# A two-layer pooling and attention block on one core: another order of the attention's last products

## The chip, the core and the metric

The kernel runs on one core of a Trainium2 chip. Its engines run side by side, each through a queue of its own: TensorE (PE: matrix products into PSUM; PEld is its loading of weights), VectorE (DVE), ScalarE (ACT), GpSimd (POOL), and DMA queues (SP issues most transfers). The metric is the device time of one execution in microseconds (us), as the median of several runs. The profile is of one execution of its own; its span goes from the first to the last instruction.

## The reference

What is computed, for one sequence of 256 tokens with 1024 features, in float32, cut to its core:

```python
x = x + pool_mixer(rmsnorm(x, norm_mixer[0]), pool_w[0], pool_scale[0])   # running means over 2, 4, 8, 16 tokens
x = x + swiglu(rmsnorm(x, norm_ffn[0]), w_gate_up[0], w_down[0])          # d_ff = 2816
k, v = split(rmsnorm(x, kv_norm) @ w_kv)                                  # 16 heads of 64
q = rmsnorm(x, norm_mixer[1]) @ w_q[0]
o = softmax(q @ k.T / 8 + bias_by_distance, causal) @ v                   # block 256: all keys are in the own block
x = x + o @ w_o[0]
x = x + swiglu(rmsnorm(x, norm_ffn[1]), w_gate_up[1], w_down[1])
return rmsnorm(x, final_norm)
```

## The kernel before, in words

Activations lie with features on the 128 partitions, as `x[128, 8, 256]`: eight tiles of features by 256 tokens. Products are made in float32r out of halves: each operand is split into a high half (a rounded copy, made by ScalarE) and a low half (the rest, made by VectorE), and `mm3` sums three products, high by high (L72), high by low (L73) and low by high (L74). `mm2` makes the same three products in two matmuls, one of 512 columns (L79) and one of 256 (L80).

**Weights.** A plan lists all pieces of weights (1024 columns each) in the order of their use: ..., kq (two for each of the eight pairs of heads), wo (one for each of eight output tiles), gu1 (two for each of 22 gate and up tiles), dn1. A piece is loaded by SP, then split by ScalarE (L65, `whi`) and VectorE (L66, `wlo`) into one of five pairs of buffers (`HALVES = 5`). When TensorE's program comes to piece i, `weights` has the split of piece i + 4 written into the program; a split has to wait until the piece five places earlier is no longer used.

**Attention.** For each pair of heads p: `project(p)` makes keys and queries (eight k steps of six matmuls; L420, L425 and L427 then scale and split them), `scores(p)` makes q k, adds the bias (L447), and takes exponentials, sums and quotients (L450, L452, L455), `turn(p)` transposes the probabilities (L467) and splits them (L470, L471), `values(p)` multiplies them by v and splits the result into `oparts` (L484 the high half, L486 the low half). These stages are staggered: while pair p is projected, the scores of p - 1, the transposes of p - 2 and the values of p - 3 are made, at a place inside the eight k steps that `cut` sets.

**Output.** `attend(ms, ks)` adds, for each output tile m and pair k, the product of the wo piece of m with pair k's `oparts`. An output tile holds a PSUM bank and its split wo piece from its first k to its last. After k = 7, L501 adds the tile to `x`, L203 and L204 make the high and low half of the scaled `x` for the second feed-forward block, L196 squares it, and L198 adds the square to a running sum (tile 0 starts the sum, so there are seven L198).

**After that** the second feed-forward block runs over j = 0 to 21 (gate and up tiles) and k = 0 to 7. After the step j = 1, k = 1 TensorE multiplies the running sum of squares by a column of 1/1024 (L177, the mean square for the norm); VectorE adds epsilon (L169), GpSimd takes the power, and after j = 2, k = 0 the factor is spread over the partitions. L286 and L287 take a finished gate tile out of PSUM.

**Order.** TensorE's order is that of the code, written out by hand. On the other engines a scheduler sets the order when the program is built, with its own estimates of times; `high_priority` moves some instructions ahead. At run time each engine goes through its list in order.

Of the kernel before, what the change touches and what calls it, by code (L numbers as in the profile page):

```python
# [16 lines left out]
KT = D // P  # L17
# [19 lines left out]
def yoco_kernel(ctx, tc, x0, xs, pool_w, kq, wv, wo, rel_bias, gu, dn, onehot, mask, out):  # L37
# [10 lines left out]
    def bank():  # L48
        return psum.tile([P, 512], F32, name="bank", tag="bank")
# [19 lines left out]
    def mm3(o, w, a, first, last):  # L69

        (wh, wl), (ah, al) = w, a
        nc.tensor.matmul(o, wh, ah, start=first, stop=False)  # L72
        nc.tensor.matmul(o, wh, al, start=False, stop=False)  # L73
        nc.tensor.matmul(o, wl, ah, start=False, stop=last)  # L74
# [36 lines left out]
    def weights(name, key):  # L111
        i = used["n"]
        assert plan[i][:2] == (name, key), (plan[i][:2], name, key)
        used["n"] += 1
        prepare(i + HALVES)
        return ready.pop((name, key))
# [74 lines left out]
    def square(tag, m, eng=None):  # L191

        sq = work.tile([P, T], F32, name="sq", tag="sq")
        if m == 0:
            sq = acc[tag] = work.tile([P, T], F32, name="acc", tag="acc")
        nc.scalar.activation(sq, x[:, m, :], AF.Square)  # L196
        if m:
            (eng or nc.vector).tensor_tensor(acc[tag], acc[tag], sq, op=ALU.add)  # L198

    def split_x(m, v, s):  # L200

        g = vec[:, v, m:m + 1]
        nc.scalar.activation(act_hi[s][:, m, :], x[:, m, :], AF.Copy, scale=g)  # L203
        nc.vector.scalar_tensor_tensor(act_lo[s][:, m, :], x[:, m, :], g, act_hi[s][:, m, :].bitcast(F32),  # L204
                                       op0=ALU.mult, op1=ALU.subtract)
# [196 lines left out]
    def project(p, ks):  # L402
        if ks[0] == 0:
            proj[p] = [bank(), bank()]
        a = proj[p]
        for k in ks:
            if k % 4 == 0:
                kqw[0] = weights("kq", (p, k // 4))
            wh, wl = kqw[0]
            for u, s in enumerate("ab"):  # L410
                c = slice(k % 4 * T + u * P, k % 4 * T + (u + 1) * P)
                mm3(a[u][:, :T], (wh[:, c], wl[:, c]), (act_hi[s][:, k, :], act_lo[s][:, k, :]), k == 0, k == KT - 1)
        if ks[-1] != KT - 1:
            return
        t = work.tile([P, 2, T], F32, name="ev", tag="ev")
        q = [work.tile([P, T], F32R, name=f"q{s}", tag=f"q{s}") for s in "hl"]
        ks = kparts[p % 2]
        with tc.high_priority(URGENT):
            for u in (1, 0):
                nc.vector.tensor_tensor(t[:, u, :], a[u][:, :T], R2[:, u, :], op=ALU.mult)  # L420
            parts = [(q[0], q[1], t[:, 1, :])]
            for f, c in ((slice(0, 64), slice(0, T)), (slice(64, P), slice(T, 2 * T))):
                parts.append((ks[0][f, c], ks[1][f, c], t[f, 0, :]))
            for hi, lo, src in parts:
                nc.scalar.activation(hi, src, AF.Copy)  # L425
            for hi, lo, src in parts:
                nc.vector.tensor_tensor(lo, src, hi.bitcast(F32), op=ALU.subtract)  # L427
        kqs[p] = q, ks

    def scores(p):  # L430
        (qh, ql), (kh, kl) = kqs.pop(p)
        a = [bank(), bank()]
        kh0, kl0 = (v.rearrange("p (b k) -> p b k", b=2)[:, :, :P] for v in (kh, kl))
        mm3(a[0][:, :T], (qh[:, :P], ql[:, :P]), (kh0, kl0), True, True)
        mm3(a[1], (qh[:, P:], ql[:, P:]), (kh, kl), True, True)
        sn = work.tile([P, 2, 3 * P], F32, name="sn", tag="sn")
        pr = work.tile([P, 2, 3 * P], F32, name="pr", tag="pr")
        mx = work.tile([P, 2, 2], F32, name="mx", tag="mx")
        sm = work.tile([P, 2, 2], F32, name="sm", tag="sm")
        iv = work.tile([P, 2, 2], F32, name="iv", tag="iv")  # L440
        cols = (slice(0, P), slice(P, 3 * P))

        with tc.high_priority(URGENT):
            for b in range(2):
                h = 2 * p + b
                for t, (src, add) in enumerate(((a[0][:, b * P:(b + 1) * P], table[:, h, P:T]), (a[1][:, b * T:(b + 1) * T], table[:, h, :]))):
                    nc.vector.tensor_tensor_reduce(sn[:, b, cols[t]], src, add, -1.0, 3.0e38, ALU.add, ALU.min, mx[:, b, t:t + 1])  # L447
            for b in range(2):
                for t in range(2):
                    nc.scalar.activation(pr[:, b, cols[t]], sn[:, b, cols[t]], AF.Exp, bias=mx[:, b, t:t + 1], scale=-1.0,  # L450
                                         accum_out=sm[:, b, t:t + 1])
            nc.vector.reciprocal(iv, sm)  # L452
            for b in range(2):
                for t in range(2):
                    nc.gpsimd.tensor_scalar(pr[:, b, cols[t]], pr[:, b, cols[t]], iv[:, b, t:t + 1], 1.0, op0=ALU.mult, op1=ALU.mult)  # L455
        probs[p] = pr
# [3 lines left out]
    def turn(p):  # L460
        pr = probs.pop(p)
        c = [bank(), bank()]
        ph, pl = (work.tile([P, 2, 3 * P], F32R, name=f"p{s}", tag=f"p{s}", bufs=1) for s in "hl")
        for b in range(2):
            for i in range(3):

                nc.tensor.transpose(c[b][:, i * P:(i + 1) * P], pr[:, b, i * P:(i + 1) * P], ident)  # L467
        with tc.high_priority(URGENT):
            for b in range(2):
                nc.scalar.activation(ph[:, b, :], c[b][:, :3 * P], AF.Copy)  # L470
                nc.vector.tensor_tensor(pl[:, b, :], c[b][:, :3 * P], ph[:, b, :].bitcast(F32), op=ALU.subtract)  # L471
        pts[p] = ph, pl

    def values(p):
        ph, pl = pts.pop(p)
        o = bank()
        ob = o.rearrange("p (b q) -> p b q", b=2)
        for t, ks, dst in ((0, slice(0, T), ob), (1, slice(T, 3 * P), ob[:, :, P:])):
            vh, vl = (v[:, t, p * P:(p + 1) * P] for v in vparts)
            mm3(dst, (vh, vl), (ph[:, :, ks], pl[:, :, ks]), t == 0, t == 1)  # L480
        with tc.high_priority(URGENT):
            fs = [slice(64 * b, 64 * b + 64) for b in range(2)]
            for b, f in enumerate(fs):
                nc.scalar.activation(oparts[0][f, p, :], ob[f, b, :], AF.Copy)  # L484
            for b, f in enumerate(fs):
                nc.vector.tensor_tensor(oparts[1][f, p, :], ob[f, b, :], oparts[0][f, p, :].bitcast(F32), op=ALU.subtract)  # L486
# [3 lines left out]
    def attend(ms, ks):  # L490
        for k in ks:
            for m in ms:
                if m not in wos:
                    wos[m] = weights("wo", (m, 0))
                    wo_out[m] = bank()
                c = slice(k * P, (k + 1) * P)
                mm3(wo_out[m][:, :T], (wos[m][0][:, c], wos[m][1][:, c]), (oparts[0][:, k, :], oparts[1][:, k, :]),
                    k == 0, k == PAIRS - 1)
                if k == PAIRS - 1:
                    with tc.high_priority(URGENT):  # L500
                        nc.vector.tensor_tensor(x[:, m, :], wo_out[m][:, :T], x[:, m, :], op=ALU.add)  # L501
                        split_x(m, V_FFN1, "a")
                    square("ffn1", m)

    for p in range(PAIRS):
        cut = 4 if p > 2 else 6
        project(p, range(cut))
        if p >= 3:
            values(p - 3)
        if p >= 1:  # L510
            scores(p - 1)
        if p >= 2:
            turn(p - 2)
        project(p, range(cut, KT))

    attend((0,), range(5))
    values(PAIRS - 3)
    turn(PAIRS - 2)
    scores(PAIRS - 1)
    attend((0,), (5,))  # L520
    attend((1,), range(6))
    values(PAIRS - 2)
    attend((2,), range(6))
    turn(PAIRS - 1)
    attend((3,), range(6))
    values(PAIRS - 1)
    attend((0, 1, 2, 3), (6,))
    attend((0, 1, 2, 3), (7,))
    for m in range(4, KT):
        attend((m,), range(KT))  # L530

    last = const.tile([P, 2, KT, T], F32, name="last", tag="table")
# [97 lines left out]
```

## Time and profile before

| | before |
|---|---|
| median of 3 runs | 516.49 us (516.49 to 516.61) |
| the profiled execution | 516.71 us |
| its span | 515.0 us |
| around the span | 1.71 us |
| TensorE busy | 506.3 us, 98% |
| VectorE busy | 398.7 us, 77% |
| ScalarE busy | 303.3 us, 59% |
| mean granted TensorE clock | 0.997 |

The profiled execution is 0.22 us above the median. The end of a matmul is modelled in the profile and matmuls overlap, so what a stretch of matmuls takes is read from their starts. The attention's projections begin at about 229 us of the span, the first product of `attend` is at 292.3, the second feed-forward block begins at about 321.2.

### The profile page before, as it was taken

What the parts mean: (1) busy time and instruction counts of PE and PEld (TensorE: products, weight loads), DVE (VectorE), ACT (ScalarE), POOL (GpSimd) and SP (SyncE); (2) the same over time, 40 slices, a digit from 0 to 9 for tenths busy, and PEclk for the clock granted to TensorE, in tenths of its full rate; (3) what the DMA queues carried; (4) which work ended last, traced back from release to release, by engine and by line L of the source; (5) the groups of instructions that cost most, each with busy time, mean ns of one, the idle gap of its engine ahead of it and who ended that gap; (6) DMA issues with size and microseconds to landing.
All of it is one profiled execution on the core that took longest, in us unless ns stands there. A gap on an engine that the chain in (4) does not pass through costs nothing.

```text
span 515.0 us, 8445 instructions
## 1 busy us (share of the span) xinstructions
PE 506.3 (98%) x3084; PEld 450.9 (88%) x3084; DVE 398.7 (77%) x730; ACT 303.3 (59%) x556; POOL 43.9 (9%) x76
## 2 busy tenths in 40 slices
PE   8999999999999999999999999999999999999995
PEld 7888888888888888889999999888888888888895
DVE  6899878988876766657989849898888888865641
ACT  3967556565655554557777739576556565544421
POOL 4230300000000000201242410000000000000000
PEclk9999999999999999999999999999999999999998
DMA  8676999655657666565524215855555565666402
GB/s 295 244 221 170 226 215 340 208 184 176 185 159 206 183 192 215 186 196 168 156 93 158 92 39 166 263 184 187 186 197 184 188 188 164 189 179 191 114 1 82
DMA packets 26810, 92.28 MB, mean 179 GB/s; under 512 B 3088, under 2 KB 3248, under 8 KB 26768
## 3 DMA queue, kind: packets, MB, share of 16 engines
q1 hardware_dynamic: 25776, 88.78, 55.1%
q0 software_dynamic: 848, 2.57, 2.8%
q8 instruction: 24, 0.39, 0.3%
q10 hardware_dynamic: 144, 0.39, 0.2%
q14 instruction: 18, 0.15, 0.1%
HBM read 90.29 MB, written 1.44 MB: 178 GB/s over the span
## 4 chain that ended last, share of the span: by engine, by line
PE 56%; issue 36%; DVE 5%; DMA 1%; ACT 1%; POOL 0%; SPq 0%; POOLq 0%; DVEq 0%
PE bank L79 24%; PE bank L80 12%; PE bank L73 6%; PE bank L74 6%; PE bank L72 6%; DVE wlo L66 2%; PE bank L467 1%; DMA x<-in_xs 1%; DVE acta L204 1%; DVE acc L198 0%; DVE x L501 0%; ACT early L225 0%; DVE early L233 0%; PE bank L177 0%; PE bank L245 0%
## 5 line engine op out<-in xcount | busy, mean ns | idle before, releaser
L66 DVE TENSOR_TENSOR wlo<-raw,whi 128x1024 fp32r<-128x1024 f32 x168 | 202.5, 1206 | 59.6 <-ACT whi L65 52.2
L65 ACT ACTIVATE whi<-raw 128x1024 fp32r<-128x1024 f32 x168 | 174.0, 1037 | 116.5 <-PE bank L79 88.5
L79 PE MATMUL bank<-actb,whi 128*128 128x512 f32 x352 | 124.4, 396 | 0.0
L79 PE MATMUL bank<-acta,whi 128*128 128x512 f32 x352 | 123.6, 394 | 0.0
L79 PE MATMUL bank<-big,whi 128*128 128x512 f32 x330 | 114.5, 390 | 0.0
L80 PE MATMUL bank<-actb,wlo 128*128 128x256 f32 x352 | 98.2, 279 | 0.0
L80 PE MATMUL bank<-acta,wlo 128*128 128x256 f32 x352 | 98.2, 279 | 0.0
L80 PE MATMUL bank<-big,wlo 128*128 128x256 f32 x330 | 93.0, 282 | 0.0
L79 PEld LDWEIGHTS bank<-actb,whi 128*128 128x128 f32 x352 | 66.0, 187 | 16.2 <-DVE ev L287 0.6
L79 PEld LDWEIGHTS bank<-acta,whi 128*128 128x128 f32 x352 | 66.0, 187 | 15.6
L79 PEld LDWEIGHTS bank<-big,whi 128*128 128x128 f32 x330 | 61.9, 188 | 13.0
L80 PEld LDWEIGHTS bank<-actb,wlo 128*128 128x128 f32 x352 | 66.0, 188 | 0.0
L80 PEld LDWEIGHTS bank<-acta,wlo 128*128 128x128 f32 x352 | 66.0, 187 | 0.0
L80 PEld LDWEIGHTS bank<-big,wlo 128*128 128x128 f32 x330 | 62.4, 189 | 0.0
L286 ACT ACTIVATE ev<-bank 128x256 f32<-128x256 f32 x88 | 33.2, 379 | 47.6 <-PE bank L80 47.6
L287 DVE TENSOR_TENSOR ev<-bank,ev 128x256 f32<-128x256 f32 x88 | 36.8, 419 | 13.1 <-ACT ev L286 13.1
L288 DVE TENSOR_TENSOR ev<-ev,R 128x256 f32<-128x256 f32 x88 | 36.8, 423 | 2.6
L455 POOL TENSOR_SCALAR pr<-pr,iv 128x128 f32<-128x128 f32 (+1 forms) x32 | 21.1, 677 | 68.0 <-DVE iv L452 40.1
L73 PE MATMUL bank<-big,whi 128*128 128x256 f32 x86 | 24.1, 281 | 0.2 <-DVE big L486 0.2
L72 PE MATMUL bank<-big,whi 128*128 128x256 f32 x86 | 24.1, 280 | 0.0
L74 PE MATMUL bank<-big,wlo 128*128 128x256 f32 x86 | 24.0, 279 | 0.0
L291 DVE TENSOR_TENSOR h<-sg,ev 128x256 f32<-128x256 f32 x44 | 18.5, 423 | 4.8 <-ACT sg L289 0.5
(135 smaller groups left out, 674.5 us busy)
## 6 DMA issues: line engine op xcount, KB each, us to landing
raw<-in_gu SPq DMA_DIRECT2D x88, 512.0 KB, 4.1
raw<-in_dn SPq DMA_DIRECT2D x32, 512.0 KB, 3.6
raw<-in_kq SPq DMA_DIRECT2D x16, 512.0 KB, 4.4
raw<-in_dn SPq DMA_DIRECT2D x16, 384.0 KB, 3.6
raw<-in_wv SPq DMA_DIRECT2D x8, 512.0 KB, 4.3
raw<-in_wo SPq DMA_DIRECT2D x8, 512.0 KB, 3.5
table<-rows POOLq DMA_DIRECT2D x8, 256.0 KB, 16.9
early<-in_pool_w SPq DMA_DIRECT2D x4, 256.0 KB, 4.8
```

The lines of the kernel that those rows point to most:

```text
L65: nc.scalar.activation(hi[:, :cols], raw[:, :cols], AF.Copy)
L66: nc.vector.tensor_tensor(lo[:, :cols], raw[:, :cols], hi[:, :cols].bitcast(F32), op=ALU.subtract)
L72: nc.tensor.matmul(o, wh, ah, start=first, stop=False)
L73: nc.tensor.matmul(o, wh, al, start=False, stop=False)
L74: nc.tensor.matmul(o, wl, ah, start=False, stop=last)
L79: nc.tensor.matmul(o, wh, a.rearrange("p a t -> p (a t)"), start=first, stop=False)
L80: nc.tensor.matmul(o[:, :T], wl, a[:, 0, :], start=False, stop=last)
L286: nc.scalar.activation(t[:, u, :], a[u][:, T:], AF.Copy)
L287: nc.vector.tensor_tensor(t[:, u, :], a[u][:, :T], t[:, u, :], op=ALU.add)
L288: nc.vector.tensor_tensor(t[:, u, :], t[:, u, :], R, op=ALU.mult)
L291: nc.vector.tensor_tensor(h, sg, t[:, 1, :], op=ALU.mult)
L455: nc.gpsimd.tensor_scalar(pr[:, b, cols[t]], pr[:, b, cols[t]], iv[:, b, t:t + 1], 1.0, op0=ALU.mult, op1=ALU.mult)
```

## The change

```diff
     for p in range(PAIRS):
-        cut = 4 if p > 2 else 6
+        cut = 4 if p > 3 else 6
         project(p, range(cut))
         if p >= 3:
             values(p - 3)
...
         project(p, range(cut, KT))
 
-    attend((0,), range(5))
+    attend((0, 1), range(5))
     values(PAIRS - 3)
     turn(PAIRS - 2)
     scores(PAIRS - 1)
-    attend((0,), (5,))
-    attend((1,), range(6))
+    attend((0, 1), (5,))
+    attend((2,), range(6))
     values(PAIRS - 2)
-    attend((2,), range(6))
+    attend((3,), range(6))
     turn(PAIRS - 1)
-    attend((3,), range(6))
+    attend((0, 1, 2, 3), (6,))
     values(PAIRS - 1)
-    attend((0, 1, 2, 3), (6,))
-    attend((0, 1, 2, 3), (7,))
-    for m in range(4, KT):
+    attend((4,), range(7))
+    attend((0, 1, 2, 3, 4), (7,))
+    for m in range(5, KT):
         attend((m,), range(KT))
```

In the loop only the pass p = 3 changes: it makes six k steps of its projection, not four, before the values of pair 0, the scores of pair 2 and the transposes of pair 1. In the straight part two output tiles instead of one are begun before `values(5)`; tile 2 and tile 3 each move one place ahead; the products with pair 6 stand before `values(7)`; a fifth tile makes seven products behind `values(7)`, and five tiles end together instead of four. All products are the same in number, form and kind.

The scheduler places VectorE's and ScalarE's work anew. Three places of that follow. In the names a number tells tiles of one kind apart.

The first is VectorE's list where the first output tiles are added to `x`. Before:

```order
L486 TENSOR_TENSOR big_2193<-bank_3454,big_2193 64x256 x2
L501 TENSOR_TENSOR x_71<-bank_3284,x_71 128x256
L501 TENSOR_TENSOR x_71<-bank_3360,x_71 128x256
L501 TENSOR_TENSOR x_71<-bank_3396,x_71 128x256
L66 TENSOR_TENSOR wlo_3355<-raw_2993,whi_3354 128x1024
L204 SCALAR_TENSOR_TENSOR acta_134<-x_71,acta_134 128x256 x3
L501 TENSOR_TENSOR x_71<-bank_3435,x_71 128x256
L66 TENSOR_TENSOR wlo_3391<-raw_3036,whi_3390 128x1024
```

And of the change:

```order
L486 TENSOR_TENSOR big_2193<-bank_3466,big_2193 64x256 x2
L501 TENSOR_TENSOR x_71<-bank_3284,x_71 128x256
L501 TENSOR_TENSOR x_71<-bank_3294,x_71 128x256
L501 TENSOR_TENSOR x_71<-bank_3385,x_71 128x256
L66 TENSOR_TENSOR wlo_3289<-raw_2993,whi_3288 128x1024
L66 TENSOR_TENSOR wlo_3380<-raw_3036,whi_3379 128x1024
L204 SCALAR_TENSOR_TENSOR acta_134<-x_71,acta_134 128x256 x3
L501 TENSOR_TENSOR x_71<-bank_3421,x_71 128x256
```

`raw_2993` and `raw_3036` are the wo pieces of tiles 5 and 6: both splits stand now before the first L204, where one did.

The second is VectorE's list around the end of the sum of squares. `sq_3658` is the square of tile 7, the last one; `wlo_3713` is the split of gu piece 6 (tile j = 3, first half), `wlo_3689` that of gu piece 5. Before:

```order
L198 TENSOR_TENSOR acc_3484<-acc_3484,sq_3621 128x256
L66 TENSOR_TENSOR wlo_3667<-raw_3394,whi_3666 128x1024
L198 TENSOR_TENSOR acc_3484<-acc_3484,sq_3658 128x256
L66 TENSOR_TENSOR wlo_3689<-raw_3433,whi_3688 128x1024
L287 TENSOR_TENSOR ev_3781<-bank_3664,ev_3781 128x256
L66 TENSOR_TENSOR wlo_3713<-raw_3517,whi_3712 128x1024
L169 TENSOR_SCALAR rv_3729<-bank_3726 128x2
```

And of the change:

```order
L66 TENSOR_TENSOR wlo_3689<-raw_3419,whi_3688 128x1024
L198 TENSOR_TENSOR acc_3512<-acc_3512,sq_3621 128x256
L66 TENSOR_TENSOR wlo_3713<-raw_3481,whi_3712 128x1024
L198 TENSOR_TENSOR acc_3512<-acc_3512,sq_3658 128x256
L287 TENSOR_TENSOR ev_3781<-bank_3664,ev_3781 128x256
L169 TENSOR_SCALAR rv_3729<-bank_3726 128x2
```

The last L198 stood before the splits of gu pieces 5 and 6; it stands behind both now, and the first L287 behind both too, where it stood between them.

The third is ScalarE's list at the same place; `bank_3664` is the first gate tile of the feed-forward block. Before:

```order
L65 ACTIVATE whi_3666<-raw_3394 128x1024
L196 ACTIVATE sq_3621<-x_71 128x256
L203 ACTIVATE acta_134<-x_71 128x256
L196 ACTIVATE sq_3658<-x_71 128x256
L65 ACTIVATE whi_3688<-raw_3433 128x1024
L286 ACTIVATE ev_3781<-bank_3664 128x256
L65 ACTIVATE whi_3712<-raw_3517 128x1024
L286 ACTIVATE ev_3781<-bank_3665 128x256
```

And of the change:

```order
L65 ACTIVATE whi_3688<-raw_3419 128x1024
L196 ACTIVATE sq_3584<-x_71 128x256
L196 ACTIVATE sq_3621<-x_71 128x256
L286 ACTIVATE ev_3781<-bank_3664 128x256
L65 ACTIVATE whi_3712<-raw_3481 128x1024
L196 ACTIVATE sq_3658<-x_71 128x256
L286 ACTIVATE ev_3781<-bank_3665 128x256
```

The square of tile 7 stood before the high halves of gu pieces 5 and 6 and before the first L286; it stands behind them now.

## Rows read from the trace of the kernel before

**Rows 1.** The page's first part: busy us, share of the span and instructions.

```profile
PE 506.3 (98%) x3084; PEld 450.9 (88%) x3084; DVE 398.7 (77%) x730; ACT 303.3 (59%) x556; POOL 43.9 (9%) x76
```

**Rows 2.** List of waits, weight loads: total us, times, longest.

```profile
PEld bank L73 <- DVE big L427: 0.5, 2, 0.3
...
PEld bank L73 <- DVE big L486: 0.4, 1, 0.4
```

**Rows 3.** Timeline, TensorE, third pair's scores: start, duration, engine, line, instruction.

```profile
253.34 0.28 PE L72 MATMUL bank<-big,qh 128*128 128x256 f32 x1
253.63 0.39 PE L73 MATMUL bank<-big,qh 128*128 128x256 f32 x1
253.86 0.28 PE L74 MATMUL bank<-big,ql 128*128 128x256 f32 x1
```

**Rows 4.** Timeline, TensorE: last pair's scores, and products behind the last transposes.

```profile
295.69 0.36 PE L72 MATMUL bank<-big,qh 128*128 128x256 f32 x1
...
296.38 0.28 PE L74 MATMUL bank<-big,ql 128*128 128x256 f32 x1
...
303.43 0.36 PE L72 MATMUL bank<-big,whi 128*128 128x256 f32 x1
303.64 0.28 PE L73 MATMUL bank<-big,whi 128*128 128x256 f32 x1
```

**Rows 5.** Timeline, TensorE, from the first product with the last values.

```profile
308.06 0.28 PE L72 MATMUL bank<-big,whi 128*128 128x256 f32 x1
308.58 0.39 PE L73 MATMUL bank<-big,whi 128*128 128x256 f32 x1 [0.24 <-DVE big L486]
308.80 0.28 PE L74 MATMUL bank<-big,wlo 128*128 128x256 f32 x1
...
313.47 0.28 PE L72 MATMUL bank<-big,whi 128*128 128x256 f32 x1
```

**Rows 6.** By stretches: length, busy us of PE, PEld, DVE, ACT, POOL, clock, DMA.

```profile
313.00:317.00 4.00, 4.00 (x37) 4.00 (x36) 4.00 (x8) 4.00 (x9) 0.00 (x0) 1.00 0.70 232
```

**Rows 7.** Timeline, VectorE, from the first tile's addition to the first L287.

```profile
309.11 1.13 DVE L501 TENSOR_TENSOR x<-bank,x 128x256 f32<-128x256 f32 x3 [0.59 <-PE bank L74]
310.16 1.21 DVE L66 TENSOR_TENSOR wlo<-raw,whi 128x1024 fp32r<-128x1024 f32 x1
...
326.23 0.41 DVE L198 TENSOR_TENSOR acc<-acc,sq 128x256 f32<-128x256 f32 x1
326.57 1.21 DVE L66 TENSOR_TENSOR wlo<-raw,whi 128x1024 fp32r<-128x1024 f32 x1
327.70 0.41 DVE L287 TENSOR_TENSOR ev<-bank,ev 128x256 f32<-128x256 f32 x1
```

**Rows 8.** Timeline, ScalarE, the same stretch.

```profile
309.00 1.06 ACT L65 ACTIVATE whi<-raw 128x1024 fp32r<-128x1024 f32 x1 [1.37 <-PE bank L73]
...
326.62 0.39 ACT L286 ACTIVATE ev<-bank 128x256 f32<-128x256 f32 x1 [1.51 <-PE bank L80]
```

**Rows 9.** Timeline, TensorE, the statistics.

```profile
328.17 0.50 PE L177 MATMUL bank<-mean,acc 128*128 128x1 f32 x4
```

**Rows 10.** VectorE's and TensorE's timelines: pair 3's low half, its use; last values.

```profile
260.86 1.07 DVE L427 TENSOR_TENSOR big<-ev,big 64x256 fp32r<-64x256 f32 x2
...
262.26 0.28 PE L73 MATMUL bank<-big,qh 128*128 128x256 f32 x1
...
306.55 0.28 PE L74 MATMUL bank<-ph,big 128*128 128x256 f32 x1
...
307.66 0.86 DVE L486 TENSOR_TENSOR big<-bank,big 64x256 fp32r<-64x256 f32 x2 [2.67 <-ACT big L484]
```

**Rows 11.** TensorE's last matmuls, and stretches to the end (columns as in Rows 6).

```profile
507.82 1.29 PE L552 MATMUL bank<-ident,last 128*128 128x128 f32 x10
...
511.00:512.00 1.00, 0.00 (x0) 0.00 (x0) 0.00 (x0) 0.00 (x0) 0.00 (x0) 0.99 1.04 404
512.00:513.00 1.00, 0.00 (x0) 0.00 (x0) 0.00 (x0) 0.00 (x0) 0.00 (x0) 0.50 1.04 412
```

## Prediction

> **What bounds the kernel now.** The page is read first [rows 1]: TensorE is busy for 506.3 of 515.0 us, so time is gained or lost only where TensorE waits. The list of TensorE's waits comes next. Near the attention it holds three, all at L73, the first product of a group that needs a low half: two for the low half of k, which L427 writes, and one for the low half of the attention output, which L486 writes [rows 2]. TensorE's timeline then gives what each costs, from the starts of consecutive matmuls. Undisturbed, 40 matmuls of 256 columns go from 308.80 to 313.47, 0.117 us each [rows 5].
> - Third pair's scores: 253.34 to 253.86 is 0.52 us for two steps that take 0.23 undisturbed. Cost 0.29 [rows 3].
> - Last pair's scores: 295.69 to 296.38, 0.69. The first step after a block of transposes takes 0.21 even without a wait (303.43 to 303.64), so 0.33 is the undisturbed time and 0.36 the cost [rows 4].
> - Seventh products after the last values: 308.06 to 308.80, 0.74 against 0.23. Cost 0.50 [rows 5].
>
> Together 1.15 us. That is the most that the three edits can give back, and just over 0.2% of 516.5 us (1.03 us), about what a measurement of this kernel can tell from no change.
>
> Then the other engines, from 309 us on. VectorE is busy for 4.00 us of 313 to 317 [rows 6]; it works without a gap from its first L501 at 309.11 to its first L287 at 327.70 [rows 7]. In that block stand 8 L501 (output added to x), 8 L204 (low half of the next activation), 7 L198 (sum of squares) and 9 L66 (low halves of weights: wo 5 to 7, gu pieces 0 to 5). The sum of squares is the operand of L177 at 328.17 [rows 9]. The last L198 ends at 326.64, so the sum is there 1.5 us before TensorE comes to L177; everything behind that matmul stands in the same queue. This margin is the place that decides.
>
> **The change, part by part.** No instruction is added or removed on TensorE; only places change.
>
> *Third pair, cut 6 for 4.* Two k steps (12 matmuls, 1.40 us) go ahead of values(0) and scores(2), so the wait of 0.29 goes. But scores(2) and turn(1) now come 1.40 us later against the end of project(3), and VectorE's work for them is pushed against L420 and L427 of pair 3. Before, that low half ends at 261.93 and is wanted at 262.26, a margin of 0.33 [rows 10]. Following ACT and VectorE through the new order (two L447, L486, two L447, L471, L452, L420, L66, L427), I get it ready about 0.1 us after it is wanted, which with the restart below costs about 0.2. Bounds of the gain: 0 and 0.29; I take 0.1.
>
> *Two tiles ahead of the last scores.* Fifteen matmuls (1.76 us) of tile 1 move ahead, past a wait of 0.36, which goes. Behind the scores there is then less between values(5) and its use in attend((0, 1), (5,)). The low half of the last values was there at 308.52 (L486 runs 0.86 from 307.66), 1.9 us after the step of their last matmul, which starts at 306.55 [rows 10]; values(5) is followed by 1.84 us of transposes, scores and one product. So about 0.1 may be waited here, and 0.1 more for the restart. Bounds 0.16 and 0.36; I take 0.2. Together **G = 0.3**, between 0.16 and 0.65.
>
> *Fifth tile between values(7) and its use.* Seven products of tile 4, 21 matmuls or 2.46 us, replace a wait of 0.50. The wait goes, as the low half is ready 1.9 us after the values. But tile 0's last product, and with it the start of VectorE's block, moves from 308.80 to 308.80 + 2.46 - 0.50 = 310.76 (less G), 1.96 later. And there are only five buffers of split weights, all held now by tiles 0 to 4: wo 5 can be split only after tile 0's last product, as before, where ScalarE starts it at 309.00 [rows 8]. Before, tile 4's eight steps (2.8 us) lay between that and tile 5. Now only the last products of tiles 1 to 4 do.
>
> *First new wait, tile 5.* VectorE starts at 311.07, does three L501 (1.05 us, 309.11 to 310.16 [rows 7]), then the L66 of wo 5 (1.21): 313.33. TensorE wants the low half five steps after tile 0's last matmul, at 310.76 + 5 x 0.352 = 312.52. It waits 0.9, plus 0.1: after a wait, the next matmul comes 0.22 later instead of 0.117 [rows 3, 5].
>
> *Second new wait, the statistics.* VectorE's block starts 1.96 later, at 311.07, and the order shows one more L66 in it (gu piece 6) before the last L198: 1.13 us (326.57 to 327.70 [rows 7]). It ends at 311.07 + 18.59 + 1.13 = 330.79; with the overlap of neighbours (0.07), the release (0.06) and the restart (0.1), TensorE is 331.02 - 328.17 = 2.85 us later behind L177 than before, less G. The wait at tile 5 is inside this sum, not beside it: VectorE's block doesn't wait for tiles 5 to 7 in my following of it, and TensorE itself reaches L177 at about 328.6, so it stands there some 2.3 us.
> The second bound drops the backlog. In the new order ScalarE has L286 of the first gate tile, then L65 of gu piece 6, ahead of the last square, and that L65 needs a buffer free that TensorE holds until the first gate tile ends. From L286's start (326.62 before [rows 8]): 0.39 + 1.06 + 1.21 + 0.41 = 3.07 until the sum is there, where L177 comes 1.55 after it. That alone is a stall of 1.5, on top of 0.97 at tile 5 and less 0.50 and G: 2.0 - G with 0.1 for the restart. Both lie on the same side; I take the first, as VectorE's queue is full.
>
> After L177 nothing gives this back: the list of TensorE's waits has none later in the program at which spare time could be absorbed, and the order of all engines there is as before.
>
> Sum against the profiled execution: 516.71 + 2.85 - 0.3 = 519.26. The median shown is 0.22 below that execution: **519.0**.
>
> The Trainium skill (Perfetto Trace Analysis, Identifying the Most-Contended Engine) has the engine of highest occupancy optimized first, by closing its gaps; over the span that is TensorE with 98% against VectorE's 77%, and by this the change would give 1.15 us, 515.3. The rows of the stretch differ: there VectorE has no idle time at all.
>
> **The rivals.**
> - *Faster.* The three waits go and nothing takes their place: 516.49 - 1.15 = 515.3. TensorE would come to L177 at 328.17 - 1.15 = 327.0 and need the sum by then, 3.6 us earlier than I get it (330.9 - G). For it: all of this is in the shade of TensorE's own work on average. Against it: the added L66 stands ahead of the last L198 in the order, and both bounds exclude it.
> - *No change.* The wait at tile 5 comes but the statistics are in time: -1.15 + 0.97 = -0.2, 516.3. It needs a VectorE block shorter by the 2.3 us of the stall: each of its ten L66 would have to take 0.9 instead of 1.13.
> - *The clock falls.* At the end of the program the last matmuls end at 509.11 and the granted clock stays at 1.00 until about 511.98, then is 0.50 (1.2 of 2.4 GHz) until the end, 3.0 us [rows 11]. A stall of 2.3 us is shorter than those 2.9, so I expect no fall. If it fell for such 3.0 us, it would cost half of them: 519.0 + 1.5 = 520.5. The Trainium skill (TensorE: Matmul & The Clock Gate, HAM oscillation) tells of kernels whose waits between bursts of matmuls put TensorE back to half its clock, each time; that speaks for this rival.
> - *The early waits come back whole* (G = 0): 519.3; kept whole (G = 0.65): 518.7. Both are within the forecast.
>
> **How the numbers follow.** Forecast 0.80, clock 0.07, no change 0.08, faster 0.05. The forecast's own range is 518.1 (the second bound, 2.0 - 0.65 = 1.35 up, is 517.8; with half of the backlog 518.1) to 519.4 (G = 0); instructions on VectorE a little slower than in the rows would add 0.2. To leave out no more than 2 in 10 I give 517.8 to 519.7. Slower by over 0.2%: 0.87; within: 0.08; faster: 0.05.
>
> **What would show it.** In the profile after: TensorE's waits list holds L177 <- VectorE L198 with some 2.3 us, and L74 <- L66 with about 0.9; L73 <- L486 is gone; the wait at the third pair's scores has moved to the fourth's or is gone. VectorE is without a gap from its first L501 to the last L198, 19.7 us. The clock is 1.00 behind L177. I am wrong if L177 starts within 0.5 us of the matmul before it: then the last L198 was not late, and either VectorE ran its block faster or the buffers were freed in another order than I read.

## The result, and the profile after

The changed kernel takes 520.94 us (median of 6 runs, 519.02 to 521.59) against 516.49 before (6 runs, 516.39 to 516.97). The ratio is 1.0076, 95% interval 1.0064 to 1.0087: slower by 0.76%, 4.4 us. The direction and the two new waits came as forecast; the time lies 1.2 us above the range.

The page of the profiled execution (520.91 us, span 519.2), first part, answers to [rows 1]: the work is the same, 1.7 us more of TensorE's time is spent on it, and the rest of the 4.2 us is standing.

```profile
PE 508.0 (98%) x3084; PEld 452.2 (87%) x3084; DVE 399.8 (77%) x730; ACT 303.4 (58%) x556; POOL 44.0 (8%) x76
```

The list of TensorE's waits (total us, times, longest) has two new lines, each at the place forecast:

```profile
PE bank L177 <- DVE acc L198: 2.1, 1, 2.1
...
PE bank L74 <- DVE wlo L66: 0.7, 1, 0.7
PE bank L73 <- DVE big L427: 0.2, 1, 0.2
```

Before, L73 <- L486 was the only line of that list from 230 us on, with 0.2; it is gone. [rows 2] show the list of weight loads, and there the line is left with half of its 0.4. It now belongs to the products with pair 5, and no longer to the last values:

```profile
PEld bank L73 <- DVE big L486: 0.2, 1, 0.2
```

TensorE's timeline at the two, answering to [rows 5] and [rows 9]. The third product of tile 5 comes 0.99 us after the second (0.117 undisturbed), the next one 0.22 later: 0.97 lost. L177 comes 2.39 us after the matmul before it.

```profile
312.18 0.28 PE L73 MATMUL bank<-big,whi 128*128 128x256 f32 x1
313.17 0.39 PE L74 MATMUL bank<-big,wlo 128*128 128x256 f32 x1 [0.71 <-DVE wlo L66]
313.39 0.28 PE L72 MATMUL bank<-big,whi 128*128 128x256 f32 x1
...
328.33 0.28 PE L80 MATMUL bank<-acta,wlo 128*128 128x256 f32 x1
330.72 0.66 PE L177 MATMUL bank<-mean,acc 128*128 128x1 f32 x4 [2.10 <-DVE acc L198]
331.23 0.78 PE L79 MATMUL bank<-acta,whi 128*128 128x512 f32 x1
331.81 0.41 PE L80 MATMUL bank<-acta,wlo 128*128 128x256 f32 x1
332.02 0.63 PE L79 MATMUL bank<-acta,whi 128*128 128x512 f32 x1
332.45 0.41 PE L80 MATMUL bank<-acta,wlo 128*128 128x256 f32 x1
332.66 0.63 PE L79 MATMUL bank<-acta,whi 128*128 128x512 f32 x1
```

The last four rows show something else: a pair of L79 and L80 takes 0.64 us there, where it takes 0.35 undisturbed (the L80 before the first row starts at 327.98, the first row at 328.33). The stretches of the same trace (length, busy us of PE, PEld, DVE, ACT, POOL, granted clock, DMA) say why: TensorE is idle from 328.6 to 330.7 with the clock at 1.00, and the clock is at 0.50, 1.2 of 2.4 GHz, from 331.1 (the 0.86 of the second stretch) to 334.5, after TensorE has gone back to work.

```profile
328.60:330.70 2.10, 0.01 (x1) 0.00 (x0) 2.10 (x5) 0.20 (x1) 0.00 (x0) 1.00 0.86 250
330.70:331.30 0.60, 0.58 (x5) 0.59 (x5) 0.30 (x1) 0.00 (x0) 0.00 (x0) 0.86 0.83 239
331.30:334.50 3.20, 3.20 (x11) 2.72 (x11) 0.97 (x4) 0.53 (x1) 0.70 (x1) 0.50 0.88 307
334.50:336.00 1.50, 1.50 (x11) 1.32 (x10) 0.94 (x1) 0.53 (x1) 0.00 (x0) 0.98 0.09 38
```

Some 3.4 us at half clock are 1.7 us of work lost, as an estimate. By the starts it is 1.6: the five pairs from 331.23 to 334.57 take 3.34 us, and 1.76 undisturbed. Of the six executions four have a mean granted clock of 0.993 to 0.995 and times of 520.91 to 521.59; the other two have 0.996 and 0.997 and take 519.02 and 519.68. So the time has two levels, near 519.3 and near 521.2, and the median is of the upper one.

VectorE's timeline answers to [rows 7]: the block starts at 310.85, and the last L198 stands behind the split of gu piece 6. From the first L501 to the end of the last L198 it takes 19.8 us, with no gap over 0.06.

```profile
310.85 1.13 DVE L501 TENSOR_TENSOR x<-bank,x 128x256 f32<-128x256 f32 x3 [1.17 <-PE bank L74]
...
329.10 1.22 DVE L66 TENSOR_TENSOR wlo<-raw,whi 128x1024 fp32r<-128x1024 f32 x1
330.24 0.42 DVE L198 TENSOR_TENSOR acc<-acc,sq 128x256 f32<-128x256 f32 x1
330.57 0.42 DVE L287 TENSOR_TENSOR ev<-bank,ev 128x256 f32<-128x256 f32 x1
```

The wait at the third pair's scores of [rows 3] is gone (254.58 to 254.82 is 0.24 for two steps), and one stands at the fourth's, where [rows 10] had none: 261.66 to 262.33 is 0.67 for two steps of 0.23, a loss of 0.44. The last pair's scores no longer wait (297.40 to 297.73 is 0.33, as undisturbed), but the first products with pair 5 behind them do: 298.55 to 298.96, 0.41 for 0.23, a loss of 0.18.

```profile
261.66 0.28 PE L72 MATMUL bank<-big,qh 128*128 128x256 f32 x1
262.11 0.38 PE L73 MATMUL bank<-big,qh 128*128 128x256 f32 x1 [0.16 <-DVE big L427]
262.33 0.28 PE L74 MATMUL bank<-big,ql 128*128 128x256 f32 x1
...
298.55 0.28 PE L72 MATMUL bank<-big,whi 128*128 128x256 f32 x1
298.74 0.38 PE L73 MATMUL bank<-big,whi 128*128 128x256 f32 x1
298.96 0.28 PE L74 MATMUL bank<-big,wlo 128*128 128x256 f32 x1
```

### The profile page after: what moved, and what is told of

Read it like the earlier page. It is cut to its first block, busy times and chain, and to the rows that moved or that the text cites. A ratio compares the mean times of both kernels' runs of the same rounds, so it can differ in the third digit from the quotient of the medians.

```text
span 519.2 us, 8447 instructions
## 1 busy us (share of the span) xinstructions
PE 508.0 (98%) x3084; PEld 452.2 (87%) x3084; DVE 399.8 (77%) x730; ACT 303.4 (58%) x556; POOL 44.0 (8%) x76
## 4 chain that ended last, share of the span: by engine, by line
PE 61%; issue 35%; DVE 2%; ACT 1%; POOL 0%; POOLq 0%; DVEq 0%
PE bank L79 24%; PE bank L80 12%; PE bank L73 7%; PE bank L74 7%; PE bank L72 7%; PE bank L467 1%; PE bank L142 1%; PE bank L220 1%; DVE wlo L66 0%; ACT early L225 0%; PE bank L177 0%; DVE acc L198 0%; PE bank L245 0%; DVE last L569 0%; POOL r_mix L171 0%
## 5 line engine op out<-in xcount | busy, mean ns | idle before, releaser
L79 PE MATMUL bank<-acta,whi 128*128 128x512 f32 x352 | 125.1, 397 | 0.0
L79 PE MATMUL bank<-actb,whi 128*128 128x512 f32 x352 | 124.4, 395 | 0.0
L79 PE MATMUL bank<-big,whi 128*128 128x512 f32 x330 | 114.5, 390 | 0.0
L80 PE MATMUL bank<-acta,wlo 128*128 128x256 f32 x352 | 98.8, 281 | 0.0
L80 PE MATMUL bank<-actb,wlo 128*128 128x256 f32 x352 | 98.2, 279 | 0.0
L80 PE MATMUL bank<-big,wlo 128*128 128x256 f32 x330 | 93.0, 282 | 0.0
L79 PEld LDWEIGHTS bank<-acta,whi 128*128 128x128 f32 x352 | 66.8, 190 | 16.0
L79 PEld LDWEIGHTS bank<-actb,whi 128*128 128x128 f32 x352 | 66.0, 187 | 16.0 <-DVE ev L287 0.6
L79 PEld LDWEIGHTS bank<-big,whi 128*128 128x128 f32 x330 | 61.9, 188 | 13.0
L80 PEld LDWEIGHTS bank<-acta,wlo 128*128 128x128 f32 x352 | 66.7, 189 | 0.0
L80 PEld LDWEIGHTS bank<-actb,wlo 128*128 128x128 f32 x352 | 66.0, 187 | 0.0
L286 ACT ACTIVATE ev<-bank 128x256 f32<-128x256 f32 x88 | 33.2, 379 | 50.4 <-PE bank L80 50.4
L80 PEld LDWEIGHTS bank<-big,wlo 128*128 128x128 f32 x330 | 62.4, 189 | 0.0
L287 DVE TENSOR_TENSOR ev<-bank,ev 128x256 f32<-128x256 f32 x88 | 36.9, 421 | 14.9 <-ACT ev L286 14.9
L73 PE MATMUL bank<-big,whi 128*128 128x256 f32 x86 | 24.1, 281 | 0.0
```

The costliest lines, as they stand in the source:

```text
L79: nc.tensor.matmul(o, wh, a.rearrange("p a t -> p (a t)"), start=first, stop=False)
L80: nc.tensor.matmul(o[:, :T], wl, a[:, 0, :], start=False, stop=last)
L286: nc.scalar.activation(t[:, u, :], a[u][:, T:], AF.Copy)
L287: nc.vector.tensor_tensor(t[:, u, :], a[u][:, :T], t[:, u, :], op=ALU.add)
```

## The experiments

The theory (queue): VectorE's work behind the output tiles is one full block; started 1.96 us later and with one more split ahead of the last L198, it gives the sum of squares too late, TensorE stands at L177, and the clock falls because of that standing. The rivals: the five held weight buffers are the cause (buffers), or the clock falls from something else in the change (clock by itself). The kernel before took 516.6 to 516.7 us in the three groups of runs below (21 runs each).

**L177 four steps later.**

```diff
-        stats = (0, KT - 1) if l == 0 else (1, 1)
-        scale = (2, KT - 3) if l == 0 else (2, 0)
+        stats = (0, KT - 1) if l == 0 else (1, 5)
+        scale = (2, KT - 3) if l == 0 else (2, 2)
```

> The changed kernel with the mean-square product L177 four k steps later (after j = 1, k = 5 instead of k = 1) and the spreading of the factor two steps later. Theory (queue): all of the loss behind the tile 5 wait comes from TensorE standing 2.3 us at L177 for the last L198, and the fall of the clock follows from that standing. Four steps are 2.8 us, so the wait goes, the clock stays at 1.00 and the time is about 516.9 (before 516.5, plus 0.97 at tile 5, plus 0.15 at the fourth pair, less 0.50 and 0.2 for the waits that went). Rival (buffers): the five held weight buffers delay all later splits, so the wait comes back at the next piece of weights: 518.5 or more. Rival (clock by itself): the clock falls without the wait at L177: about 518.5, with a mean clock near 0.994.

Measured: 517.05 us (11 runs), ratio 1.0008 (0.9999 to 1.0017). No wait at L177, no fall of the clock, and none came at the next weights. The list of waits from 230 us on keeps the other two lines:

```profile
PE bank L74 <- DVE wlo L66: 0.7, 1, 0.7
PE bank L73 <- DVE big L427: 0.2, 1, 0.2
```

**The sum earlier instead.**

```diff
                         split_x(m, V_FFN1, "a")
-                    square("ffn1", m)
+                        square("ffn1", m)
```

> The changed kernel with the squares and their additions (L196, L198) given the same priority as the additions to x, so that the last L198 stands behind five splits in VectorE's list instead of ten. L177 stays where it is. Queue theory: the sum is there by about 325, before TensorE comes; no wait at L177, no fall of the clock, about 516.9, as when L177 is moved. Buffers: the splits are no earlier, so 518.5 or more. Clock by itself: 518.5.

Measured: 517.22 us (11 runs), ratio 1.0011 (1.0002 to 1.0019). L177 follows the matmul before it (328.65) at once:

```profile
328.76 0.50 PE L177 MATMUL bank<-mean,acc 128*128 128x1 f32 x4
```

Two edits that have nothing in common but the distance between the last L198 and L177 take away the same 3.7 to 3.9 us. Both keep the change's order of products, its five held buffers and its wait at tile 5.

**Six buffers.**

```diff
-RAWS, HALVES = 6, 5
+RAWS, HALVES = 5, 6
```

> The changed kernel with six pairs of buffers for split weights (and five for unsplit ones, for the room). The split of wo 5 no longer waits for tile 0. Queue theory: the wait of 0.97 at tile 5 goes, but VectorE's block has ten splits before the last L198 as it had, so the sum comes at the same time, TensorE arrives earlier and the wait at L177 grows to some 3.2 us: the time stays at 519.0 without a fall of the clock and 520.9 or a little more with it. Buffers: both waits go, about 515.9. If the two waits simply add: 520.0 with the fall, 518.0 without.

Measured: 522.58 us (4 runs, 521.96 to 523.22). The wait at tile 5 is gone, and that at L177 has grown by about as much:

```profile
PE bank L177 <- DVE acc L198: 3.0, 1, 3.0
PE bank L73 <- DVE big L427: 0.2, 1, 0.2
```

The sum comes at 331.8 here, 1.1 later than in the change. That is from further ahead: the first transposes come 1.1 later already (248.23 against 247.12), and in the first layer this kernel's L177 waits 0.7 us for GpSimd's L198 and 0.7 for VectorE's L234, lines that the change's list does not have. VectorE's block itself takes 19.8 us from 311.97, as in the change. So the two new waits are one loss: what is not waited at tile 5 is waited at L177. The rival of the buffers falls by this: with a sixth the kernel is no faster. The time is 1.7 above the 520.9 expected, and the 1.1 explain most of it. Two of the four executions have a mean clock of 0.991, lower than any of the change, and take 523.2; the profiled one, with 0.994, takes 522.0. Where the two lost more, no profile shows.

**L177 one step later.**

```diff
-        stats = (0, KT - 1) if l == 0 else (1, 1)
+        stats = (0, KT - 1) if l == 0 else (1, 2)
```

> The changed kernel with L177 one k step later (0.70 us), nothing else moved. Queue theory: the wait there is 1.6 instead of 2.3 us, and as the steps behind L177 are only shifted, 518.3 if the clock doesn't fall, 519.9 if it does. If the fall is set by the length of the standing, fewer runs fall than of the changed kernel (four of six there were near 521, two near 519). Clock by itself: the same share of falls as there.

Measured: 518.59 us (5 runs). One step of 0.70 us takes 0.7 off the wait. The profiled execution is the one whose clock fell, 520.21; the others have 518.42, 518.47, 518.59 and 519.25, at clocks of 0.997 to 0.999.

```profile
330.74 0.61 PE L177 MATMUL bank<-mean,acc 128*128 128x1 f32 x4 [1.41 <-DVE acc L198]
```

**The cut alone.**

```diff
-        cut = 4 if p > 2 else 6
+        cut = 4 if p > 3 else 6
```

> The kernel before with the later scores of the third pair alone. Theory from the profile of the change: the wait of 0.29 at the third pair's scores goes, and one of 0.33 with 0.10 of restart comes at the fourth's, since VectorE gets to the low half of k of pair 3 later: +0.15 us against before. Rival: the wait goes and nothing comes: -0.29.

Measured: 516.65 us (11 runs), ratio 0.9999 (0.9991 to 1.0008). The time can't tell +0.15 from -0.29; the trace can: the wait stands at the fourth pair's scores, as in the change, and its second matmul comes 0.46 us after the first.

```profile
261.54 0.28 PE L72 MATMUL bank<-big,qh 128*128 128x256 f32 x1
262.00 0.39 PE L73 MATMUL bank<-big,qh 128*128 128x256 f32 x1 [0.17 <-DVE big L427]
```

**The fifth tile alone.**

```diff
     attend((0, 1, 2, 3), (6,))
-    attend((0, 1, 2, 3), (7,))
-    for m in range(4, KT):
+    attend((4,), range(7))
+    attend((0, 1, 2, 3, 4), (7,))
+    for m in range(5, KT):
```

> The kernel before with tile 4's seven products behind the last values and five tiles ending together, nothing else. Queue theory: this edit alone makes the loss. VectorE's block starts 1.96 us later with one more split ahead of the last L198: waits of 0.97 at tile 5 and 2.3 to 2.5 at L177, 519.2 where the clock stays and 521 where it falls. Rival: the edits lose only together (five tiles and the earlier start of tiles 2 and 3): no more than tile 5's 0.97 less 0.50, 517.0.

Measured: 521.13 us (4 runs, clocks of 0.993 and 0.994), ratio 1.0088 (1.0074 to 1.0101). This one edit holds the whole loss, with the same two waits:

```profile
PE bank L177 <- DVE acc L198: 2.0, 1, 2.0
PE bank L74 <- DVE wlo L66: 0.7, 1, 0.7
```

**The change without the cut.**

```diff
-        cut = 4 if p > 3 else 6
+        cut = 4 if p > 2 else 6
```

> The changed kernel with the third pair's scores where they were before. If the cut is worth +0.15 alone it is worth that here too: 0.15 below the changed kernel (519.0 where the clock stays, 520.8 where it falls). Otherwise 0.29 above it.

Measured: 520.61 us (5 runs): three at 520.61 to 521.29 with clocks of 0.993 and 0.994, two at 519.66 and 519.75 with 0.997. The two levels hide a difference of 0.15, so the time settles nothing on the cut; it shows the two levels a second time, 0.86 us apart at the least (519.75 and 520.61). The trace does tell: the third pair's scores lose 0.28 again (253.74 to 254.25 for two steps), and the fourth's, which lose 0.44 in the change, lose nothing (262.53 to 262.77). The difference, 0.16, is the one expected.

**Two steps of tile 4 instead of seven.**

```diff
     attend((0, 1, 2, 3), (6,))
+    attend((4,), range(2))
     attend((0, 1, 2, 3), (7,))
-    for m in range(4, KT):
+    attend((4,), range(2, KT))
+    for m in range(5, KT):
```

> The kernel before with only two of tile 4's products (0.70 us) between the products with pair 6 and those with pair 7, its other six behind tile 3. Queue theory: 0.70 is more than the wait of 0.50 that stood there, so this goes; VectorE's block starts only 0.2 later, has as many splits ahead of the last L198 as before, the margin at L177 shrinks from 1.5 to 0.8, and tile 5's split has six steps to hide behind: 0.50 less than before, 516.0. Rival: any work put ahead of tile 0's last product is paid for at L177 or tile 5: no gain, 516.5 or more.

Measured: 516.14 us (11 runs), ratio 0.9992 (0.9983 to 1.0001): 0.5 below the 516.64 of before in the same runs, at the edge of what can be told. In the trace TensorE no longer waits for L486, and it waits neither at tile 5 nor at L177.

**A late sum in the kernel before.**

```diff
                     square("ffn1", m)
+                    if m == KT - 1:
+                        with tc.high_priority(URGENT):
+                            for i in range(3):
+                                nc.vector.tensor_tensor(acc["ffn1"], acc["ffn1"], acc["ffn1"], op=ALU.max)
```

> The kernel before, its attention untouched, with three additions of VectorE (the greater of the sum and itself, which leaves the sum as it is) behind the last L198 and ahead of L177's operand. Between them stand the splits of gu pieces 5 and 6, as in the change. Queue theory: the sum is there at 330.3 instead of 326.6, TensorE stands 2.1 us at L177, and this alone gives most of the loss: 518.8 where the clock stays, 520.4 where it falls, some runs at each. Rival (clock by itself, or by the wait at tile 5): the clock never falls here, all runs near 518.8.

Measured: 520.29 us (5 runs), ratio 1.0073 (1.0061 to 1.0086): four at 520.06 to 520.84 with clocks of 0.993 and 0.994, one at 519.45 with 0.997. The wait, and two of the stretches (columns as above): TensorE is idle through 328 to 329, works from 329.9, and the clock is at 0.50 behind it.

```profile
PE bank L177 <- DVE acc L507: 2.0, 1, 2.0
```

```profile
328.00:329.00 1.00, 0.00 (x0) 0.00 (x0) 1.00 (x2) 0.00 (x0) 0.00 (x0) 1.00 0.84 262
...
331.00:332.00 1.00, 1.00 (x5) 0.80 (x4) 0.47 (x2) 0.00 (x0) 0.50 (x1) 0.50 0.93 258
```

None of the change's edits is in this kernel, no product is moved, and tile 5 waits for nothing. A sum that comes 3.2 us later (its last operation ends at 329.86, where L198 ended at 326.64) gives the loss of the change within 0.7 us, the fall of the clock with it. Both halves of the theory are shown by this run, and the clock by itself is out.

**Two versions with the waits of before removed.**

```diff
-        cut = 4 if p > 2 else 6
+        cut = 4 if p > 3 else 5 if p > 2 else 6
...
-    attend((0,), range(5))
+    attend((0, 1), range(5))
     values(PAIRS - 3)
     turn(PAIRS - 2)
     scores(PAIRS - 1)
-    attend((0,), (5,))
-    attend((1,), range(6))
+    attend((2,), range(3))
+    attend((0, 1), (5,))
+    attend((2,), range(3, 6))
     values(PAIRS - 2)
-    attend((2,), range(6))
+    attend((3,), range(4))
     turn(PAIRS - 1)
-    attend((3,), range(6))
+    attend((3,), (4, 5))
+    attend((0, 1), (6,))
     values(PAIRS - 1)
-    attend((0, 1, 2, 3), (6,))
+    attend((2, 3), (6,))
+    attend((4,), range(4))
     attend((0, 1, 2, 3), (7,))
-    for m in range(4, KT):
+    attend((4,), range(4, KT))
+    for m in range(5, KT):
```

together with L177 after j = 1, k = 5, as in the first experiment:

> A version that should beat both: five k steps ahead of the third pair's scores (not four or six), tiles 0 and 1 ahead of the last scores, three steps of tile 2 between these and pair 5's products, four steps of tile 4 split off and put behind the last values, the others behind tile 3, and L177 after j = 1, k = 5. Queue theory: all three waits of before go (1.15 us), tile 5's split has seven steps to hide behind, and L177 comes late enough for one more split ahead of the sum: 515.3 to 515.6. Rival: one of the waits comes back elsewhere: 516 to 516.5.

Measured: 515.45 us (11 runs), ratio 0.9979 (0.9970 to 0.9988), 1.1 below the 516.57 of before in the same runs. From 230 us on its list of waits is empty, for matmuls and for loads of weights.

The smaller one, two steps of tile 4 and the cut at five:

> The kernel before with two of tile 4's products ahead of those with pair 7, and five k steps ahead of the third pair's scores. Half the shift of the change leaves the fourth pair's low half 0.3 us in time and gives the third's 0.7 us more: the wait of 0.29 goes and none comes. With the 0.50 of the two steps 0.79 below before: 515.7. Rival: the wait moves to the fourth pair as it does with six: 516.0 or more.

Measured: 515.86 us (11 runs), ratio 0.9987 (0.9978 to 0.9996). One wait is left, that of the last pair's scores, which this version doesn't touch:

```profile
PE bank L73 <- DVE big L427: 0.2, 1, 0.2
```

## Why the prediction was right and wrong

**The price of each old wait** (0.29, 0.36, 0.50) was right: with all three gone the kernel is 1.1 us faster, where the sum was 1.15, and the 0.50 alone gave 0.5, at the edge of what can be told.

**The third pair** was mis-sized. I took a gain of 0.1, and called 0 its lower bound. The wait moved to the fourth pair, as described, and cost 0.44 there instead of 0.2: a loss of 0.15. The low half of pair 3's k was 0.3 us late, not 0.1. Halving the shift shows that the place was right: with a cut of five the wait at the third pair goes and none comes.

**Two tiles ahead of the last scores**: the wait of 0.36 went and 0.18 came back at the products with pair 5, so 0.18 gained where I took 0.2. G is then 0.03 instead of 0.3, and outside its bounds of 0.16 to 0.65.

**Tile 5** was forecast at 0.9 plus 0.1 and measured at 0.97, and six buffers showed that it stands inside the sum.

**The statistics** came as forecast. Forecast: VectorE's block 19.72 us, a stand of some 2.3 us. Measured: 19.8, and 2.39 from the matmul before L177 to L177, of which 0.12 is the matmul's own step. This trace runs 0.2 us ahead of that of before already at 247 us (247.12 against 247.33 for the same transposes), so L177 is 2.55 + 0.21 = 2.76 us later; 2.85 less G less the restart behind it gives 2.72 with the measured G. The level that was forecast, 519.0, and 519.3 with that G, is the one that two of six runs have (519.02 and 519.68).

**The step that failed** is the rival "the clock falls", with its chance of 0.07 and the sentence "A stall of 2.3 us is shorter than those 2.9, so I expect no fall". [rows 11] show how long after its last matmul the clock was still at 1.00; I read that as how long TensorE must stand before the clock falls, and so the range, which ends at 519.7, has no room for a fall. The runs show otherwise. The 2.9 is not even a fixed length: from the end of the last matmul to the fall at the end of the program it is 1.8 us in the run with L177 four steps later, 2.1 in the change and 4.2 in the run with two steps and the cut at five. Nor did going back to work prevent the fall. In the change the clock falls 2.5 us after TensorE stops (328.6 to 331.1), when it has been back at work for 0.4 us. Without the cut it falls 1.8 us after the return. With L177 one step later TensorE stopped at 329.3 and waited 1.4, and in that one execution the clock fell all the same.

How often it fell is read from the mean clocks and times. A stand of 2.0 to 2.1 us in the list of waits was followed by a fall in 15 of 20 runs (4 of 6 of the change, 4 of 4 with the fifth tile alone, 3 of 5 without the cut, 4 of 5 with the late sum); one of 1.4 in one of 5; one of 3.0 in 4 of 4; and the 0.7 at tile 5 alone in none of the 22 runs of the first two experiments. The price that the rival named, 1.5, was nearly right: 1.6 by the starts of the profile, 519.0 + 1.5 = 520.5 against 520.94. The Trainium skill (TensorE: Matmul & The Clock Gate, HAM oscillation) spoke for this rival. The traces agree with it in that a wait between bursts of matmuls put the clock to half, for 3.4 us. They differ from its example in two things: the waits there last some 3 to 5 us and the clock falls at each, while here 1.4 to 3.0 us were enough, and not each time.

What stays open is why one execution of a kernel falls and another doesn't. Each kernel has one profiled execution, and in every kernel with a stand at L177 that one fell; how long TensorE stood in those that did not fall is not shown.

## What to carry to other kernels

An engine that is busy 77% over the span can be full for twenty microseconds on end, and there its list, not the busiest engine, sets when results come: before work is put in front of a milestone, follow the list of the engine behind it to the next thing that the busiest engine reads from it. To hide a wait, put in little more work than the wait lasts, and spend the rest of that work where the next wait would come: with 0.70 us of work in the wait of 0.50 the kernel was 0.5 us faster, at the edge of what can be told, and with 2.46 us it was 4.5 us slower. A wait of TensorE costs more than its length where the clock falls behind it, so in this kernel a stand of two microseconds is to be priced at its own length and some 1.6 to 1.9 us more (1.6 by the starts, 1.9 between the two levels of time).

## What was not expected of the hardware

The granted clock fell after TensorE had resumed, by 0.4 to 1.8 us, and it fell behind stands of 1.4 to 3.0 us, though at the end of the program it stays at 1.00 for 2.9 us after the last matmul [rows 11]. That time is itself not fixed: 1.8 to 4.2 us over the profiles of these kernels. Each of the six profiled falls behind L177 lasted about 3.4 us at 0.50. This gave one program two levels of time, 519.0 to 519.7 and 520.9 to 521.6, of which a median shows one.
